# A 128-byte marker tile, and the output projection's weight sums taken beside the gates instead of beside the filters

## The chip, the cores and the metric

The kernel runs on one NeuronCore of a Trainium2 chip. The metric is the device time of one execution in microseconds. Three executions of the kernel before took 2389.43, 2389.97 and 2391.98 us (median 2389.97). All durations below come from one further execution that the hardware profiler recorded: it took 2390.31 us, of which 2388.5 us lie between the first and the last instruction of the program (the span), and about 1.8 us around them.

## The reference

One encoder layer is applied to two independent inputs of 1024 positions by 1024 channels, all in float32. Cut to what matters here:

```python
xn = rmsnorm(x, g_pre)
p = xn @ w_in                                    # 1024 x 8192
fv, fg, hv, hg, mg = split(p)
y_f = (fft2_real(fv) * silu(fg)) @ w_fourier_out
v, x1, x2 = split(short_conv(hv, w_short))
z = v
for n, gate in enumerate((x1, x2)):              # filters kf depend on weights only
    z = gate * (irfft(rfft(z, 2L) * kf[:, n]) + hyena_d[n] * z)
y_h = (z * silu(hg)) @ w_hyena_out
g_f, g_h = split(sigmoid(mg + b_merge))
out = (g_f * y_f + g_h * y_h) @ w_out            # the last projection
return x + rmsnorm(out, g_post)
```

The filters `kf` come from a small network with sine activations and a decay, and are the same for both inputs.

## The kernel before

**Number format.** A float32 product is made of three TensorE matmuls on rounded parts (`mm3` and `times`): each operand is split into a high part h (ScalarE rounds it in `split`, L167 to L172) and a low part l (VectorE or GpSimd subtracts, L180), and h·h, h·l and l·h are added in PSUM. So a stationary block h is used in two matmuls and its l in one. One TensorE line, L193, issues almost all of them; in the profile they are told apart by their tiles.

**Stages in order of time.** (1) The Fourier branch of both inputs, to about 200 us; it writes the normalized, transposed inputs to the DRAM buffers `d_x[b][k]`. (2) The filters (`phase_main`, 16 steps `i`, to about 672 us): each step makes the filter of 128 channels and writes its spectrum to DRAM, while TensorE computes parts of the input projection of input 0 (`spill_gate`, tile `pin`) between them. (3) The branches (`branches`, to about 1655 us): 32 steps of convolution by block Fourier transforms (tiles `pX`, `pT`), with the projections for v, x1, x2 (`pin`) between them; input 0 first, then input 1, whose projection weights come ready split from DRAM. (4) The gates of input 1 (`phase_tail`, to about 1912 us): 12 pairs of column tiles of `w_in`. (5) The nets (tile `pn`, to about 2208 us): the two branch projections, four times 28 products. (6) The rows: the last projection by `w_out` with the closing norm, eight pairs of row tiles, to the end.

**Seven products for eight.** Stages 4 to 6 multiply 2 by 2 blocks with seven block products. For that, sums of blocks of both operands are needed: T1 to T4 of the moving operand, and s1 to s4 of the stationary one. The T sums of input 1's data (for the gates) and of `w_out` (for the rows) are made long before their use and are kept in DRAM, in `d_t[0]` and `d_t[1]`. `block_sums` (L1132) makes one eighth of them: four loads of 128 x 512 values (256 KB) by SP's queue, three VectorE instructions, four stores of 256 KB by SP's queue. It is called eight times in the filter steps 3 to 10, alternately for `d_x[1]` and for `w_out`, in the two halves of a room that later holds the table `cinv`.

**Where tiles lie.** The pools of SBUF tiles lie one behind the other, and each tile takes its size rounded up to 32 bytes of a partition. In the program as built the constants' pool `cp` starts at byte 16512, which is 129 times 128. Its tiles take 512 + 32 + 64 + 192 + 288 + 64 + 64 + 32 = 1248 bytes, so the pool `wp` starts at byte 17760, which leaves 96 over a multiple of 128. `wp` holds eleven tiles of 2048 bytes, among them `wh` and `wl`, three buffers each of the projection's split weights (also used for the blocks 11 and 12 of the gates and rows), and last the tile `mark`, 4 bytes wide, which takes 32. So the next pool `xp` (the split inputs `x`, later reused for `oB`, `n` and other cells) starts at byte 40320, which is 315 times 128. All pools behind it (`mf`, `wa`, `wb`, `mi` of stages 2 and 3; `gs` with the rooms, `gw` with s1 to s4 and a2, `gr` in stages 4 to 6) hold tiles of multiples of 512 bytes, so their tiles start at multiples of 128 as well (but for the last, small pool of the rows). The tiles of the Fourier stage lie in pools that start where `wp` starts and are closed before.

**What sets the order.** Each engine works off one list in order. A planner makes the lists from the program order and modelled times; an instruction may move ahead of others on its engine when the plan has its operands ready. `issue_after` pins an instruction behind another one on the same engine. `mark` is written by a GpSimd copy of one column of a finished gate; it holds back one DMA of `weight_sums` per step of stage 3 until that step is done.

Of the kernel before, what the change touches and what calls it, by code (L numbers as in the profile page):

```python
# [10 lines left out]
F32R = mybir.dt.float32r  # L11
# [5 lines left out]
P = 128  # L17
# [143 lines left out]
class K:  # L161
# [824 lines left out]
    def phase_main(self, nct=8, nb=NB, nf=16):  # L986
        tc, nc, a = self.tc, self.nc, self.a
        with ExitStack() as es:
            pool = lambda n: es.enter_context(tc.tile_pool(name=n, bufs=1, reuse_waits="tile"))
            self.open_mm(es, "psm")  # L990
            mf, wa, wb, mi = pool("mf"), pool("wa"), pool("wb"), pool("mi")
            ws = Rooms(wa, wb)
            with tc.issue_after(self.fz_stored.ins):
                self.load_x(0, range(4))
            self.hid = ws.tile([P, L], F32R, tag="q", name="hid", bufs=2)
            hid = ws.tile([P, L], F32, tag="q", name="hidr", bufs=2)
            for i in range(2):
                nc.sync.dma_start(hid[64 * i:64 * i + 64].rearrange("p (n t) -> p n t", n=2),
                                  self.d_h.rearrange("(n p) t -> p n t", n=2))
            with tc.issue_after(self.third[0].ins), tc.issue_after(self.third[1].ins):  # L1000
                nc.scalar.copy(self.hid, hid)
                self.sub("dve", self.hid[64:128], hid[64:128], self.hid[64:128])
            taps = self.filter_taps(0, 0, self.filter_rates(0, 0, ws), ws)
            self.load_x(0, range(4, 8))
            self.cfw0 = mf.tile([P, 4 * P], F32, name="cfw0")
            self.cfwd = mf.tile([P, 2, 12 * P], F32R, name="cfwd")
            nc.sync.dma_start(self.cfw0, a["c_fw0"])
            nc.gpsimd.tensor_copy(self.cfwd[:, 0, 0:1], self.X[4][0][1][:, 0:1])
            nc.gpsimd.dma_start(self.cfwd, a["c_fwd"])
            plain = [(5, c) for c in range(8)] + [(6, c) for c in range(8)] + [(4, c) for c in range(NH)]  # L1010
            fill = sorted([((2 * c + 1) / len(plain), t) for c, t in enumerate(plain)]
                          + [((2 * c + 1) / max(NF, 1), (0, c)) for c in range(NF)])
            fill = [t for _, t in fill]
            rates = self.filter_rates(1, 0, ws)
            self.due = self.weight_sums()
            room = mi.tile([P, 2, INVW], F32, tag="cinv", name="sums", bufs=1).rearrange("p a b -> p (a b)")
            rows = [[self.d_x[1][k][:, 512 * h:512 * h + 512] for k in range(8) for h in range(2)],
                    [a["w_out"][k * P:(k + 1) * P, 512 * h:512 * h + 512] for k in range(8) for h in range(2)]]
            for i in range(nf):
                if 3 <= i < 11:  # L1020
                    u, k = (i - 3) % 2, (i - 3) // 2
                    self.block_sums(room[:, 2048 * u:2048 * u + 2048], u, k, rows[u])
                nxt = self.filter_taps((i + 1) % 2, (i + 1) // 2, rates, ws) if i + 1 < nf else None
                self.filter_spectrum(i % 2, i // 2, taps, ws)
                if i + 2 < nf:
                    rates = self.filter_rates(i % 2, i // 2 + 1, ws, self.rounded)
                taps = nxt
                for sec, c in fill[i * len(fill) // nf:(i + 1) * len(fill) // nf]:
                    self.spill_gate(0, sec, c, ws)
                if i == 12:  # L1030
                    self.cinv = mi.tile([P, 2, INVW], F32R, tag="cinv", name="cinv", bufs=1)
                    self.cin0 = mi.tile([P, 4 * P], F32, name="cin0")
                    nc.sync.dma_start(self.cin0, a["c_in0"])
                if 12 <= i < 15:

                    s = slice((i - 12) * INVW // 3, (i - 11) * INVW // 3)
                    nc.gpsimd.dma_start(self.cinv[:, :, s], a["c_inv"][:, :, s])
            self.branches(nb, nct, ws)

    def branches(self, nb, nct, ws):  # L1040

        tc, nc = self.tc, self.nc
        steps = []
        for b in range(nb):
            steps.append((b, 0, 0))
            for c in range(1, nct):
                steps += [(b, 0, c), (b, 1, c - 1)]
            steps.append((b, 1, nct - 1))  # L1050
        plain = list(self.PLAIN)
        Z, X, G = {}, {}, {}

        def front(i):
            b, n, c = steps[i]
            src = self.conv(1, c, ws, "v", b) if n == 0 else Z.pop(c)
            return self.conv_front(src, ws)

        def gates(i):
            b, n, c = steps[i]  # L1060
            x = self.conv(2 + n, c, ws, f"x{n + 1}", b)
            if n and b == 0:
                early = c < NH
                ps = None if early else self.inproj(4, c)
                sg = [self.wp.tile([P, 512], F32, tag="gt", name="sg", bufs=3) for q in range(2)]
                for q in range(2):
                    s = slice(512 * q, 512 * q + 512)
                    if early:
                        nc.sync.dma_start(sg[q], self.d_g[0][4][c][:, s])
                    else:  # L1070
                        nc.scalar.activation(sg[q], ps[:, s], AF.Silu)
                G[i] = sg, early
            X[i] = x

        def close(i):

            if i in G:
                sg, early = G.pop(i)
                for q in range(2):
                    s = slice(512 * q, 512 * q + 512)  # L1080
                    if early:
                        with tc.issue_after(self.rounded.ins):
                            nc.scalar.activation(sg[q], sg[q], AF.Silu)
                    self.mul("dve", X[i][:, s], X[i][:, s], sg[q])
        B = front(0)
        gates(0)
        for i, (b, n, c) in enumerate(steps):
            nxt = None
            if i + 1 < len(steps):
                nxt = front(i + 1)  # L1090
                gates(i + 1)
                if i + 2 < len(steps) and steps[i + 2][0] != steps[i + 1][0]:
                    self.load_x(steps[i + 2][0])
            y = self.conv_back(n, c, B, ws)
            close(i + 1)
            B = nxt
            for _ in range({4: 1, 3: 1, 2: 2, 1: 2}.get(len(steps) - i, 0)):
                self.spill_gate(b, *plain.pop(), ws)
            z = self.gate(n, c, y, X.pop(i))
            if self.due:  # L1100
                mark = self.wp.tile([P, 1], F32R, tag="mark", name="mark", bufs=1)
                with tc.issue_after(nc.gpsimd.tensor_copy(mark, z[:, 0:1]).ins):  # L1102
                    self.due.pop(0)()
            if n == 0:
                Z[c] = z
                continue
            nc.sync.dma_start(self.d_sh[b][c], z)
            if b == 0 and NF <= c:
                self.spill_gate(0, 0, c, ws)
        with tc.issue_after(self.ended.ins):  # L1110
            for sec, c in plain:
                self.spill_gate(1, sec, c, ws)
# [16 lines left out]

    PLAIN = [(5, 0), (5, 1), (6, 0), (6, 1), (5, 2), (5, 3), (6, 2), (6, 3)]  # L1130

    def block_sums(self, room, u, k, rows):  # L1132

        r = room.rearrange("p (a b) -> p a b", a=4)
        for q in range(4):
            self.nc.sync.dma_start(r[:, q], rows[2 * (k + 4 * (q // 2)) + q % 2])
        self.sub("dve", r[:, 0:2], r[:, 0:2], r[:, 1::2])
        self.stt("dve", r[:, 3], r[:, 0], -1.0, r[:, 3], MUL, SUB)
        self.add("dve", r[:, 2], r[:, 3], r[:, 2])
        for q, j in enumerate((0, 2, 3, 1)):  # L1140
            self.nc.sync.dma_start(self.d_t[u][j][:, k], r[:, q])

    def weight_sums(self):

# [25 lines left out]
    def phase_tail(self):  # L1170
# [10 lines left out]
        with ExitStack() as es:  # L1181
# [378 lines left out]
            for i, job in enumerate(gates):  # L1560
# [8 lines left out]
                if not end:  # L1569
                    A = prepared("g", *gates[i + 1])  # L1570
                    pa, pb, m1 = first(A, Y)
                    if i + 2 == len(gates):
                        step(-6)
                else:
                    act, dve = self.rounded.ins.engine, self.left.ins.engine
                    for s in range(2):
                        pinned(product, s)
                        step(s)
# [135 lines left out]
```

## Time and profile before

| | |
|---|---|
| median of three runs | 2389.97 us |
| the profiled execution | 2390.31 us, span 2388.5 us |
| TensorE matmul busy | 2341.1 us, 98% of the span |
| VectorE busy | 1971.1 us, 83% |
| ScalarE, GpSimd busy | 1110.1 us, 452.9 us |
| DMA | 479.71 MB, 201 GB/s in the mean |
| granted TensorE clock | 0.996 in the mean |

The groups of instructions give, for one line, engine, operation and set of tiles: the count, the busy time, the mean duration of one in ns, and the engine's idle time before them with what ended it. A tile left of the arrow is written, those right of it are read: in `pin<-x,wh` the moving operand is `x` and the stationary one `wh`. PE is a matmul, PEld the load of its stationary operand, which runs beside the matmul before. A matmul's duration is longer than the distance to the next one, since they are pipelined. The chain of work shows long runs of matmuls with their time and count, which gives that distance. The tables of stretches give each engine's busy time in a stretch, the granted clock, the share of time in which the DMA engines were busy, and GB/s.

### The profile page before, as it was taken

What the parts mean: (1) busy time and instruction counts of PE and PEld (TensorE: products, weight loads), DVE (VectorE), ACT (ScalarE), POOL (GpSimd) and SP (SyncE); (2) the same over time, 40 slices, a digit from 0 to 9 for tenths busy, and PEclk for the clock granted to TensorE, in tenths of its full rate; (3) what the DMA queues carried; (4) which work ended last, traced back from release to release, by engine and by line L of the source; (5) the groups of instructions that cost most, each with busy time, mean ns of one, the idle gap of its engine ahead of it and who ended that gap; (6) DMA issues with size and microseconds to landing.
All of it is one profiled execution on the core that took longest, in us unless ns stands there. A gap on an engine that the chain in (4) does not pass through costs nothing.

```text
span 2388.5 us, 36189 instructions
## 1 busy us (share of the span) xinstructions
PE 2341.1 (98%) x12784; PEld 2013.8 (84%) x12784; DVE 1971.1 (83%) x3430; ACT 1110.1 (46%) x2072; POOL 452.9 (19%) x428
## 2 busy tenths in 40 slices
PE   6999999999989999999999999999999999999998
PEld 5998888888878888888888888888888888888787
DVE  7775789888788999999888999997655578787987
ACT  6654557767653433334223232333443464556443
POOL 3342231222323333232000000112000000101311
PEclk9999999999999999999999999999999999999999
DMA  7636895555556567667464565455554678998654
GB/s 260 213 135 216 291 322 177 166 170 166 191 184 209 188 213 208 209 196 251 153 201 143 172 189 162 147 159 166 201 164 138 222 257 271 269 311 247 195 160 141
DMA packets 246208, 479.71 MB, mean 201 GB/s; under 512 B 24582, under 2 KB 82280, under 8 KB 245706
## 3 DMA queue, kind: packets, MB, share of 16 engines
q1 hardware_dynamic: 222013, 402.25, 51.8%
q0 software_dynamic: 23792, 75.11, 11.1%
q8 instruction: 101, 1.65, 0.3%
q14 instruction: 81, 0.66, 0.1%
q10 hardware_dynamic: 221, 0.04, 0.0%
HBM read 326.82 MB, written 177.73 MB: 211 GB/s over the span
## 4 chain that ended last, share of the span: by engine, by line
PE 49%; issue 5%; DVE 4%; DMA 3%; POOL 0%; ACT 0%; DVEq 0%; SPq 0%; POOLq 0%; ACTq 0%
PE pin L193 19%; PE pg L193 14%; PE pn L193 5%; PE pT L193 5%; PE pX L193 5%; DMA d_m<-gt 1%; PE tph L904 1%; DVE x L176 0%; DMA oB<-d_wo 0%; DMA g<-d_g 0%; DMA k<-d_k 0%; DVE wl L180 0%; DVE t L180 0%; POOL d_m L1359 0%; DVE gt L180 0%
## 5 line engine op out<-in xcount | busy, mean ns | idle before, releaser
L193 PE MATMUL pin<-x,wh 128*128 128x512 f32 x2816 | 901.9, 396 | 7.5 <-DVE x L176 7.5
L193 PEld LDWEIGHTS pin<-x,wh 128*128 128x128 f32 x2816 | 523.5, 188 | 119.7 <-issue 7.6
L193 PE MATMUL pin<-x,wl 128*128 128x512 f32 x1408 | 558.1, 397 | 0.0
L180 POOL TENSOR_TENSOR wl<-wr,wh 128x512 fp32r<-128x512 f32 x128 | 229.8, 1796 | 670.6 <-ACT wh L170 621.1
L193 PEld LDWEIGHTS pin<-x,wl 128*128 128x128 f32 x1408 | 265.0, 188 | 55.1
L193 PE MATMUL pn<-room,wh 128*128 128x512 f32 x864 | 266.5, 389 | 0.2 <-DVE room L180 0.2
L193 PEld LDWEIGHTS pn<-room,wh 128*128 128x128 f32 x864 | 162.1, 188 | 34.3 <-DVE room L180 0.6
L193 PE MATMUL pn<-room,wl 128*128 128x512 f32 x432 | 168.4, 390 | 0.6 <-DVE wl L180 0.5
L180 DVE TENSOR_TENSOR t<-pX,k 128x1024 f32<-128x1024 f32 x128 | 155.4, 1214 | 10.1 <-PE pX L193 6.8
L193 PE MATMUL pX<-bh,cfwd 128*128 128x256 f32 x768 | 162.2, 288 | 0.0
L193 PE MATMUL pT<-cinv,yh 128*128 128x256 f32 x768 | 145.6, 284 | 1.4 <-DVE T0s L180 1.4
L170 ACT CAST wh<-wr 128x512 fp32r<-128x512 f32 x128 | 79.1, 618 | 142.6 <-PE pin L193 106.2
L170 ACT CAST bh<-b 128x512 fp32r<-128x512 f32 x144 | 88.4, 620 | 113.2 <-DVE b L180 78.8
L193 PEld LDWEIGHTS pT<-cinv,yh 128*128 128x128 f32 x768 | 122.9, 190 | 8.6 <-ACT T1s L957 1.5
L193 PEld LDWEIGHTS pX<-bh,cfwd 128*128 128x128 f32 x768 | 127.1, 190 | 2.6
L1359 POOL DMA_DIRECT2D d_m<-gt x32 | 27.2, 849 | 536.4 <-DVE gt L180 498.1
L170 ACT CAST yh<-y 128x512 fp32r<-128x512 f32 x96 | 59.6, 621 | 126.9 <-DVE y L180 126.4
L180 DVE TENSOR_TENSOR bl<-b,bh 128x512 fp32r<-128x512 f32 x144 | 107.1, 748 | 7.8 <-ACT bh L170 7.7
L193 PE MATMUL pT<-cinv,yl 128*128 128x256 f32 x384 | 109.0, 284 | 0.0
L193 PE MATMUL pX<-bl,cfwd 128*128 128x256 f32 x384 | 109.0, 284 | 0.0
L1102 POOL CAST mark<-x 128x1 fp32r<-128x1 f32 x30 | 21.6, 720 | 411.2 <-DVE x L176 411.0
L180 DVE TENSOR_TENSOR y<-t 128x512 f32<-128x512 f32 x128 | 91.7, 717 | 7.3 <-PE pT L193 6.9
(359 smaller groups left out, 5154.4 us busy)
## 6 DMA issues: line engine op xcount, KB each, us to landing
k<-d_k SPq DMA_DIRECT2D x128, 512.0 KB, 4.2
wr<-in_w_in SPq DMA_DIRECT2D x128, 256.0 KB, 3.4
d_g<-gt SPq DMA_DIRECT2D x124, 256.0 KB, 2.8
wl<-d_s SPq DMA_DIRECT2D x56, 512.0 KB, 5.5
d_k<-kt SPq DMA_DIRECT2D x128, 128.0 KB, 2.3
d_k<-kt SPq DMA_DIRECT2D x64, 256.0 KB, 2.8
g<-d_g SPq DMA_DIRECT2D x64, 256.0 KB, 5.2
r<-d_g SPq DMA_DIRECT2D x60, 256.0 KB, 5.8
```

The source lines that it names most:

```text
L170: self.rounded = nc.scalar.copy(h, src)
L180: return e.tensor_tensor(out, a, b, op=op)
L193: return self.nc.tensor.matmul(out, lhsT, rhs, start=start, stop=stop, skip_group_check=shared)
L904: nc.tensor.transpose(tp[:, q * P:(q + 1) * P], eo[:, e, q], self.ident)
L1102: with tc.issue_after(nc.gpsimd.tensor_copy(mark, z[:, 0:1]).ins):
L1359: nc.gpsimd.dma_start(dst, t, accum_op=ADD)
```

## The change

`mark` becomes 32 values wide (128 bytes of a partition); the copy still writes one of them. `block_sums` takes its four tiles as a list and the two source rows, and does four VectorE instructions of 512 columns in place of three of 1024, 512 and 512. In the filters it is called four times, in the steps 3, 5, 7 and 9, for `d_x[1]` alone. The four calls for `w_out` move into the gates' loop of `phase_tail`, for the pairs 2 to 5, behind the first two block products of the next pair. They use four cells of `xp`, `x10` to `x13`, in which the second halves of the first four input tiles lay, and which no later gate reads.

```diff
@@ phase_main
-            rows = [[self.d_x[1][k][:, 512 * h:512 * h + 512] for k in range(8) for h in range(2)],
-                    [a["w_out"][k * P:(k + 1) * P, 512 * h:512 * h + 512] for k in range(8) for h in range(2)]]
             for i in range(nf):
-                if 3 <= i < 11:
-                    u, k = (i - 3) % 2, (i - 3) // 2
-                    self.block_sums(room[:, 2048 * u:2048 * u + 2048], u, k, rows[u])
+                if i in (3, 5, 7, 9):
+                    k = (i - 3) // 2
+                    r = room[:, 2048 * (k % 2):2048 * (k % 2) + 2048].rearrange("p (q n) -> p q n", q=4)
+                    self.block_sums([r[:, q] for q in range(4)], 0, k, [self.d_x[1][k + 4 * j] for j in range(2)])
@@ branches
-                mark = self.wp.tile([P, 1], F32R, tag="mark", name="mark", bufs=1)
-                with tc.issue_after(nc.gpsimd.tensor_copy(mark, z[:, 0:1]).ins):
+                mark = self.wp.tile([P, 32], F32R, tag="mark", name="mark", bufs=1)
+                with tc.issue_after(nc.gpsimd.tensor_copy(mark[:, 0:1], z[:, 0:1]).ins):
                     self.due.pop(0)()
@@ block_sums
-    def block_sums(self, room, u, k, rows):
-        r = room.rearrange("p (a b) -> p a b", a=4)
+    def block_sums(self, r, u, k, rows):
         for q in range(4):
-            self.nc.sync.dma_start(r[:, q], rows[2 * (k + 4 * (q // 2)) + q % 2])
-        self.sub("dve", r[:, 0:2], r[:, 0:2], r[:, 1::2])
-        self.stt("dve", r[:, 3], r[:, 0], -1.0, r[:, 3], MUL, SUB)
-        self.add("dve", r[:, 2], r[:, 3], r[:, 2])
+            self.nc.sync.dma_start(r[q], rows[q // 2][:, q % 2 * 512:q % 2 * 512 + 512])
+        self.sub("dve", r[0], r[0], r[1])
+        self.sub("dve", r[1], r[1], r[3])
+        self.stt("dve", r[3], r[0], -1.0, r[3], MUL, SUB)
+        self.add("dve", r[2], r[3], r[2])
         for q, j in enumerate((0, 2, 3, 1)):
-            self.nc.sync.dma_start(self.d_t[u][j][:, k], r[:, q])
+            self.nc.sync.dma_start(self.d_t[u][j][:, k], r[q])
@@ phase_tail, in the loop over the gates
                     A = prepared("g", *gates[i + 1])
                     pa, pb, m1 = first(A, Y)
+                    if 2 <= i < 6:
+                        r = [cell(xp, f"x1{2 * (i % 2) + j}", f"ws{j}") for j in range(2)]
+                        self.block_sums([r[q // 2][:, q % 2] for q in range(4)], 1, i - 2,
+                                        [a["w_out"][(i - 2 + 4 * j) * P:(i - 1 + 4 * j) * P] for j in range(2)])
```

## The prediction

> **What bounds the kernel now.** I read the busy times first, then what TensorE waited for, longest first.
>
> ```profile
> span 2388.5 us, 36189 instructions
> PE 2341.1 (98%) x12784; PEld 2013.8 (84%) x12784; DVE 1971.1 (83%) x3430; ACT 1110.1 (46%) x2072; POOL 452.9 (19%) x428
> ```
>
> ```profile
> PE tpx L359 <- DVE x L344: 11.6, 1, 11.6
> PE pin L193 <- DVE x L176: 7.5, 1, 7.5
> PE pft L193 <- DVE db L180: 1.1, 1, 1.1
> ```
>
> TensorE is busy for 98% of the span. Of its idle time 11.6 us lie at the start, where the change does nothing, and 7.5 us are one wait at the turn from the filters to the branches. So the time is nearly the sum of the distances between matmuls, and the view that matters is how far apart they follow each other. The groups of instructions, with shapes kept apart, show two classes among the matmuls of 512 columns:
>
> ```profile
> L193 PE MATMUL pin<-x,wh 128*128 128x512 f32 x2816 | 901.9, 396 | 7.5 <-DVE x L176 7.5
> L193 PE MATMUL pg<-x,wh 128*128 128x512 f32 x176 | 55.3, 395 | 0.0
> L193 PE MATMUL pg<-oB,wh 128*128 128x512 f32 x120 | 37.7, 395 | 0.0
> L193 PE MATMUL pg<-x,wa 128*128 128x512 f32 x24 | 5.6, 389 | 0.0
> L193 PE MATMUL pg<-x,s4h 128*128 128x512 f32 x96 | 29.5, 389 | 0.0
> L193 PE MATMUL pg<-oB,s4h 128*128 128x512 f32 x64 | 19.7, 389 | 0.0
> L193 PE MATMUL pn<-room,wh 128*128 128x512 f32 x864 | 266.5, 389 | 0.2 <-DVE room L180 0.2
> L193 PEld LDWEIGHTS pin<-x,wh 128*128 128x128 f32 x2816 | 523.5, 188 | 119.7 <-issue 7.6
> L193 PEld LDWEIGHTS pn<-room,wh 128*128 128x128 f32 x864 | 162.1, 188 | 34.3 <-DVE room L180 0.6
> ```
>
> With the same moving tile `x`, the matmul takes 395 ns with `wh` of the pool `wp` and 389 with `wa` or `s4h` of `gw`; with `oB` it is again 395 and 389. (`wh` under `pn` is another tile, in `gw` and `xp`.) The load of the stationary block takes 188 ns in both classes. The chain gives the distances: 27.76 us for 119 `pin` is 233.3 ns, 5.44 us for 24 `pg` of the other class is 226.7 ns, a difference of 6.6.
>
> ```profile
> 1659.04 27.76 PE pin L193 x119
> 1917.05 5.44 PE pg L193 x24
> ```
>
> What tells the classes apart is where the tiles lie: `wp` starts 96 bytes over a multiple of 128, and all else on a multiple. That is the link to `mark`, which shifts every pool behind `wp`.
>
> On the last point the Trainium skill speaks against any effect. Its page "SBUF — State Buffer" (section Operand start alignment, and the 16-byte cachelines of its specifications) asks only for a start at a multiple of the element size, and a shift by 32 bytes crosses no other number of 16-byte lines; its page "TensorE: Matmul & The Clock Gate" (Part 2, Step-by-step) says that loading the next weights takes no read bandwidth from the running matmul. By these pages the two classes would be one; the trace has 395 and 389 ns. The same page's distance for 512 columns (Back-to-back issue gap) would be 512/2.4 + 2.5 = 216 ns, an estimate; the trace has 226.7 and 233.3.
>
> **The change, part 1: `mark`.** Its tile takes 128 bytes for 32, so every tile behind `wp` starts 96 bytes later: 96 over a multiple of 128, as `wp`'s tiles do. The copy still writes one value and costs what it cost. No instruction is added. There are two readings of the two classes, which the trace of before can't part, since there the moving tile always lies on a multiple.
>
> Reading A: what costs 6.6 ns is that the two operands lie differently. After the change all pairs lie alike, and the `wp` class falls to 226.7. Reading B: what costs is a stationary tile off the multiple. Then the `wp` class stays, and the other class rises to 233.3. I lean to A, since the load of a `wp` block is not longer (188 and 188 ns); it is the matmul running beside it that is longer, so it looks like two streams in each other's way, and that depends on both addresses. That is an argument, not a proof.
>
> How many matmuls each reading moves, by stage (matmuls that touch `pin`, then all):
>
> ```profile
> 200.00:672.00 472.00, 363.26 (x1508) 278.04 (x1509) 0.00 (x0) 33.17 (x60) 1.00 0.66 213
> 672.00:1100.00 428.00, 278.00 (x1111) 203.28 (x1109) 58.48 (x46) 26.67 (x25) 0.99 0.65 199
> 1100.00:1655.00 555.00, 367.84 (x1483) 269.69 (x1483) 63.75 (x50) 34.35 (x37) 1.00 0.55 171
> 1655.00:1912.00 257.00, 29.43 (x125) 22.92 (x123) 0.00 (x0) 3.21 (x6) 1.00 0.56 185
> ```
>
> ```profile
> 1100.00:1655.00 555.00, 555.00 (x3275) 487.06 (x3274) 502.54 (x834) 168.46 (x306) 48.74 (x50) 1.00 0.55 171
> 1655.00:1912.00 257.00, 257.00 (x1136) 211.06 (x1135) 147.08 (x223) 105.20 (x178) 4.17 (x3) 1.00 0.56 185
> 1912.00:2208.00 296.00, 295.77 (x1304) 244.31 (x1303) 232.75 (x248) 178.51 (x232) 20.39 (x24) 1.00 0.86 271
> 2208.00:2389.00 181.00, 169.48 (x736) 137.28 (x735) 151.53 (x283) 77.14 (x159) 40.16 (x24) 0.98 0.54 166
> ```
>
> Reading A: 1508, 1111, 1483 and 125 `pin`, and in gates and rows 176 + 120 with the high part shown above and half as many with the low part, 444 in all. Times 6.6 ns: 10.0 + 7.3 + 9.8 + 0.8 + 2.9 = 30.8 us. Not all of it reaches the end, since a faster TensorE meets VectorE in the branches of input 0:
>
> ```profile
> 800.00:900.00 100.00, 100.00 (x590) 87.72 (x589) 98.06 (x155) 36.16 (x66) 41.90 (x44) 1.00 0.67 206
> 900.00:1000.00 100.00, 98.65 (x595) 86.95 (x594) 96.44 (x150) 33.41 (x60) 29.43 (x36) 1.00 0.68 210
> 1000.00:1100.00 100.00, 100.00 (x592) 87.72 (x591) 100.00 (x163) 37.46 (x70) 36.88 (x36) 1.00 0.68 196
> ```
>
> There VectorE is busy for 294.5 of 300 us, so 5.5 are left, and TensorE would need about 5 less (7.3 times 300/428). I take 3 of these as lost, and 1 more in 1100 to 1655, where VectorE has 502.5 of 555. That leaves 27. Between nothing lost and all of the 7.3 lost, the ends are 31 and 23.
>
> Reading B: of the 3176 matmuls behind 1655 us, 125 `pin` and 444 with `wp` tiles stay; the rest, some 2600, rise by 6.6 ns: 17 us more, and TensorE never waits there for long, so all of it shows.
>
> The matmuls of 256 columns I cost at nothing under both. Their durations lie close together wherever their tiles lie (the Fourier pools hold tiles at odd starts):
>
> ```profile
> L193 PE MATMUL pT<-cinv,yl 128*128 128x256 f32 x384 | 109.0, 284 | 0.0
> L193 PE MATMUL pse<-seq,oo 128*128 128x258 f32 x48 | 7.1, 283 | 0.0
> L193 PE MATMUL pso<-seq,oo 128*128 128x258 f32 x48 | 7.7, 288 | 0.7 <-DVE sst L180 0.7
> ```
>
> For 3000 of them, 1 ns either way is 3 us either way. DMAs into shifted tiles could change too; tiles of `wp` are loaded today at the same offset, so I take nothing and allow 2 us either way.
>
> **Part 2: the sums for `w_out` leave the filters.** The rows for the tile `sums`, and the stretches in which they lie:
>
> ```profile
> L180 DVE TENSOR_TENSOR sums<-sums x16: 675/950/1227, 259.3 to 333.5; 128x1024 f32<-128x1024 f32 x8, 128x512 f32<-128x512 f32 x8
> L176 DVE SCALAR_TENSOR_TENSOR sums<-sums x8: 673/682/691, 260.5 to 330.2; 128x512 f32<-128x512 f32 x8
> DMA to landing us min/median/max: 3.3/4.8/7.0
> ```
>
> ```profile
> 300.00:350.00 50.00, 48.90 (x259) 40.86 (x258) 41.81 (x84) 25.56 (x54) 14.59 (x9) 1.00 0.99 331
> 350.00:400.00 50.00, 49.54 (x277) 42.18 (x276) 48.12 (x112) 36.22 (x86) 12.78 (x7) 1.00 0.62 192
> ```
>
> Four calls go: 16 loads, 16 stores (8.4 MB) from SP's queue, and on VectorE 4 x (1.23 + 0.68 + 0.68) = 10.3 us. They go from where the DMA engines are 99% busy. But TensorE is idle there for 1.10 + 0.46 = 1.6 us only, so the gain lies between 0 and 1.6; I take 1, since the one wait that has a name (`db`, 1.1 us) is for VectorE, which they load. The four calls that stay cost 4 x 0.1 more on VectorE (four instructions of 0.68 for 2.59), hidden under TensorE's work.
>
> The wait of 7.5 us at the turn to the branches is 350 us later. VectorE was not full in between, so the missing 10 us don't pass on by themselves; but the planner lays its lists anew, and that wait may shrink to nothing or come twice: 7.5 us either way, nothing in the sum.
>
> **Part 3: they come to the gates.** Four pairs, each 19 us long (224.8 us of the chain's `pg` for 12 pairs), get 4 x 0.68 = 2.7 us on VectorE, four loads and four stores on SP's queue. VectorE is busy there for 147 of 257 us and the DMA engines for 0.56, so there is room; TensorE, busy for all of 257, is the cover. What is queued behind: on VectorE, in order, the sums hold up the evacuation of the gates' PSUM if they wait for a load; on SP's queue, a store that waits for VectorE holds up the next pair's loads of `w_in`. In the filters a load took 4.8 us to land. The cells are free from the end of the last projection, so the first two pairs' loads can go long before; only the third and fourth wait for a store. Nothing can be gained, since TensorE has no idle time there to lose. Ends: 0, and 2 x 4.8 = 10 us if VectorE stood still for both landings with no cover. I take 0.5, near the end that the row of the stretch gives.
>
> Sum on the profiled execution: 2390.3 - 27 - 1 + 0.5 = 2362.8, so 2363. That execution lies 0.3 us above the median of the runs, which changes nothing here.
>
> **The rivals.** *B, the stationary tile alone:* 2390.3 + 17 - 0.5 = 2407. For it: the stationary tile's place is all that differs between rows with the same moving tile, so it is the shorter account. Against it: the load's 188 ns. It decides as soon as the 512-column matmuls of the nets stand 233 ns apart. *C, no effect of the shift:* `wp`'s matmuls are slow for something else that stays with `wp` (its low addresses, the DMAs into it): 2390.3 - 0.5 = 2390, with the planner's 7.5 either way. For it: `wp` itself doesn't move. The pages quoted above give the same time by their own reasoning. *D, the gates become late:* the stores on SP's queue delay the loads of the third and fourth pair's successors by a landing and the sums (4.8 + 2.7 = 7.5 us each, 15 us in all); with A 2378, without it 2405. It decides once TensorE waits for more than 5 us in 1655 to 1912. Against it are the idle 110 us of VectorE there. *E, the moving tile off the multiple costs as well:* another 6.6 ns for 7250 matmuls, 2455. No row speaks for it.
>
> **How the numbers follow.** A 0.46, C 0.20, B 0.26, D 0.05, E 0.03. Likeliest: A, 2363; its own range is 2350 (nothing lost on VectorE, the wait at the turn gone) to 2378. The range over the cases must take in C and B to leave out no more than 2 in 10: 2352 to 2410. Below 0.2% (4.8 us, about what a measurement can tell from no change) under 2390: A, and a fifth of C and D: 0.51. Within: most of C, 0.16. Above: B, E, the rest of C and D: 0.33.
>
> **What would show it.** A: `pin<-x,wh` falls from 396 to 389 ns and `pg<-x,wh` with it, while `pn<-room,wh` stays at 389. B: `pn` and the s tiles rise to 395, `pin` stays. C: both stay. Part 2: no `sums` from `w_out` before 400 us, TensorE's idle time in 300 to 400 under 1.6. Part 3: tiles `ws` in the gates, TensorE still busy for all of that stretch. The prediction is wrong if the two classes don't move, or the other way; and too low if VectorE holds the branches by more than 4 us.

## The result, and the profile after

The changed kernel takes 2387.59 us (median of 22 runs, 2383.93 to 2393.20), the kernel before beside it 2391.74 (22 runs): a ratio of 0.9985, with a 95% interval of 0.9979 to 0.9990. By this ratio that is 3.6 us less, and not the 27 that I forecast. The profiled execution took 2390.22 us, 0.1 us less than the one profiled before, so its views show what moved inside the kernel and not the whole gain.

The page of the changed kernel, its span and busy times:

```profile
span 2388.4 us, 36206 instructions
PE 2339.0 (98%) x12784; PEld 2019.5 (85%) x12784; DVE 1967.7 (82%) x3438; ACT 1118.6 (47%) x2080; POOL 446.4 (19%) x428
```

By the prediction TensorE's busy time was to fall by some 27 us; it fell by 2. The groups of instructions of the changed kernel, with the two classes of 512-column matmuls of the prediction:

```profile
L193 PE MATMUL pin<-x,wh 128*128 128x512 f32 x2816 | 900.3, 395 | 0.0
L193 PE MATMUL pin<-x,wl 128*128 128x512 f32 x1408 | 556.8, 396 | 0.0
L193 PE MATMUL pn<-room,wh 128*128 128x512 f32 x864 | 266.2, 389 | 0.0
...
L193 PE MATMUL pT<-cinv,yl 128*128 128x256 f32 x384 | 108.9, 284 | 0.0
...
L193 PE MATMUL pg<-x,wh 128*128 128x512 f32 x176 | 55.3, 395 | 0.0
...
L193 PE MATMUL pg<-x,s4h 128*128 128x512 f32 x96 | 29.6, 390 | 0.0
```

`pin` was at 396 and 397 and is at 395 and 396; `pg<-x,wh` was and is at 395; the other class stays at 389 or 390. The chain of work gives the distances (start, time, count):

```profile
1659.61 27.66 PE pin L193 x119
1687.28 224.92 PE pg L193 x984
...
1917.63 5.44 PE pg L193 x24
```

27.66 us for 119 is 232.4 ns, where it was 233.3. Over 4224 `pin` that is 3.8 us, as much as the whole gain. The fast class is at 5.44/24 = 226.7 ns as before. So neither class changed sides. The rest of the change, in the views in which the prediction looked for it, the waits of TensorE first (total, times, longest):

```profile
PE tpx L359 <- DVE x L344: 11.7, 1, 11.7
PE pXf L193 <- DVE b L180: 5.5, 1, 5.5
...
PE pn L765 <- DVE acc L180: 2.2, 1, 2.2
```

The wait of 7.5 us at the turn to the branches is now one of 5.5 us by another matmul, and a wait of 2.2 us in the filters is new. Then stretches of time of the changed kernel, with the busy time of each engine, the granted clock, the DMA share and GB/s:

```profile
300.00:350.00 50.00, 50.00 (x273) 43.08 (x272) 41.22 (x98) 33.55 (x73) 13.31 (x10) 1.00 0.72 229
350.00:400.00 50.00, 50.00 (x275) 43.18 (x275) 41.52 (x99) 35.37 (x79) 9.75 (x7) 1.00 0.56 175
...
1655.00:1912.00 257.00, 257.00 (x1135) 211.48 (x1134) 156.23 (x239) 105.49 (x178) 8.51 (x3) 1.00 0.64 218
```

In the filters the DMA share fell from 0.99 to 0.72 in the stretch where it had been full, and TensorE's 1.6 us of idle time there are gone. They are not gained, though: with the new wait of 2.2 us TensorE is idle for 2.8 us in all between 205 and 672 us, where before it was 1.6. In the gates VectorE and the DMA engines carry what was added (147 to 156 us, 0.56 to 0.64), and TensorE is still busy for all of the 257 us. The moved sums themselves, tile `ws` of the changed kernel:

```profile
L180 DVE TENSOR_TENSOR ws<-ws x8: 682/684/693, 1697.4 to 1723.0; 128x512 f32<-128x512 f32 x8
...
its engine sat idle before it (us, times) until:
  DMA ws<-in_w_out: 0.9, 2
...
DMA to landing us min/median/max: 2.2/6.0/9.3
```

VectorE stood still for 0.9 us in all for their landings.

### The profile page after: what moved, and what is told of

The parts are those of the page before. It is cut to its first block, busy times and chain, and to the rows that moved or that the text cites. A ratio compares the mean times of both kernels' runs of the same rounds, so it can differ in the third digit from the quotient of the medians.

```text
span 2388.4 us, 36206 instructions
## 1 busy us (share of the span) xinstructions
PE 2339.0 (98%) x12784; PEld 2019.5 (85%) x12784; DVE 1967.7 (82%) x3438; ACT 1118.6 (47%) x2080; POOL 446.4 (19%) x428
## 4 chain that ended last, share of the span: by engine, by line
PE 55%; DVE 4%; DMA 1%; issue 1%; ACT 0%; POOL 0%; DVEq 0%; SPq 0%; POOLq 0%; ACTq 0%
PE pin L193 19%; PE pg L193 14%; PE pn L193 12%; PE pT L193 5%; PE pX L193 5%; PE tph L904 1%; DMA xr<-in_x 1%; DVE x L176 0%; DMA d_m<-gt 0%; DMA k<-d_k 0%; DVE t L180 0%; DVE b L180 0%; DVE y L180 0%; DVE wl L180 0%; DVE o L176 0%
## 5 line engine op out<-in xcount | busy, mean ns | idle before, releaser
L180 POOL TENSOR_TENSOR wl<-wr,wh 128x512 fp32r<-128x512 f32 x128 | 223.5, 1747 | 696.1 <-ACT wh L170 661.3
```

The costliest lines, as they stand in the source:

```text
L180: return e.tensor_tensor(out, a, b, op=op)
```

## The experiments

The question was why `pin` stayed slow. Theory P: what sets the pace is the difference between the starts of the stationary and the moving tile, but modulo 512 bytes, not 128. In the kernel before this difference is 32 for the `wp` class and 0 for the other; after the change it is 128 and 0. Theory W: `wp`'s matmuls are slow for something that stays with `wp` (the prediction's rival C). No kernel below leaves out or changes any part of the computation.

**Mark alone, and the sums alone.** The kernel before with part 1 only:

```diff
-                mark = self.wp.tile([P, 1], F32R, tag="mark", name="mark", bufs=1)
-                with tc.issue_after(nc.gpsimd.tensor_copy(mark, z[:, 0:1]).ins):
+                mark = self.wp.tile([P, 32], F32R, tag="mark", name="mark", bufs=1)
+                with tc.issue_after(nc.gpsimd.tensor_copy(mark[:, 0:1], z[:, 0:1]).ins):
```

> The kernel before with mark 128 bytes wide and nothing else (part 1 alone; the order of every engine's instructions is that of before; nothing is left out). Theory P (a matmul of 512 columns runs at 226.7 ns only where its stationary and its moving tile start at the same remainder modulo 512 bytes; 32 bytes apart and 128 bytes apart are both wrong): the pin matmuls stay at 232 to 233 ns, and the time is 1 to 5 us under before, as the whole of the change was (3.6 us). Theory W (the weights of wp are slow for something that stays with that pool, its place or the writes into it, and the offset means nothing): pin stays at 233.3 ns, time within 1 us of before, and the 3.6 us come from the moved sums. Reading A of the prediction (apart by a multiple of 128 is enough) would give pin at 227 ns and 2363; the result of the whole change speaks against it.

The changed kernel with that edit undone:

> The changed kernel with mark back at 4 bytes in its 32-byte slot (parts 2 and 3 alone: the sums of the weights beside the gates, those of the data beside the filters; the order of every engine's instructions is that of the changed kernel; nothing is left out). Theory P: pin at 233.3 ns as before, time within 2 us of before (the moved sums cost and gain nothing that lasts). Theory W: 3.6 us under before, like the whole change.

Measured: 2389.17 us, 0.9989 of before (0.9980 to 0.9998), and 2389.19 us, 0.9991 (0.9982 to 1.0000). The same run of `pin` in the chains, mark alone first, then the sums alone:

```profile
1656.00 27.66 PE pin L193 x119
```

```profile
1657.93 27.76 PE pin L193 x119
```

232.4 ns with the wide mark, 233.3 without, whatever the sums do. So the 0.9 ns belong to `mark`, and reading A with its multiple of 128 is out. Each half is worth some 2 us (2.6 and 2.2 by the ratios); the sum of 4.8 agrees with the 3.6 within the intervals. W's expectation, all of it from the sums, is not met by `mark`'s half. That placement can have a large effect these two runs don't show yet.

**No difference at all.** The changed kernel with `mark` in the pool of constants, ahead of `wp`: `wp` moves up by 32 bytes, and all tiles behind it start at the same remainder as its own.

```diff
-        self.ones = cp.tile([P, 2], F32, name="ones")
+        self.ones = cp.tile([P, 2], F32, name="ones"); self.mark = cp.tile([P, 1], F32R, name="mark")
...
-                mark = self.wp.tile([P, 32], F32R, tag="mark", name="mark", bufs=1)
-                with tc.issue_after(nc.gpsimd.tensor_copy(mark[:, 0:1], z[:, 0:1]).ins):
+                with tc.issue_after(nc.gpsimd.tensor_copy(self.mark, z[:, 0:1]).ins):
```

> The changed kernel with mark taken out of wp and put into the pool of constants ahead of it, so that the tiles behind wp lie at the same remainder modulo 512 as those of wp (apart by 0 instead of 128 bytes); order of instructions as in the changed kernel, nothing left out. Theory P: pin's 128x512 matmuls fall from 232.4 to 226.7 ns and their weight-load rows from 396 to 389, 4224 x 5.7 ns = 24 us, less 0 to 5 us where VectorE (94% busy in 800 to 1100 us) becomes the limit: 2364 to 2371 us, 0.988 to 0.992 of before. Theory W: pin stays at 232 to 233 ns, 2385 to 2392 us.

Measured: 2370.45 us, 0.9908 of before (0.9891 to 0.9925). Groups, chain and stretches of this kernel:

```profile
span 2362.9 us, 36206 instructions
PE 2318.3 (98%) x12784; PEld 2016.4 (85%) x12784; DVE 1966.6 (83%) x3438; ACT 1119.0 (47%) x2080; POOL 449.0 (19%) x428
...
L193 PE MATMUL pin<-x,wh 128*128 128x512 f32 x2816 | 889.0, 391 | 0.0
```

```profile
1637.86 27.00 PE pin L193 x119
1664.86 223.04 PE pg L193 x984
```

```profile
900.00:1000.00 100.00, 98.57 (x590) 87.42 (x589) 98.68 (x153) 34.35 (x64) 35.43 (x42) 1.00 0.69 208
```

The run of `pin` is at 226.9 ns and the gates begin at 1664.9 us, 22 us earlier than before. (This execution took 2364.98 us, the shortest of the four; the difference of the medians is 20.7.) W is out. The mean of all `pin` stays 2 ns above the fast class (391 to 389), which I come back to.

**A difference of 64 and of 96 bytes.** The changed kernel with a narrower mark:

```diff
-                mark = self.wp.tile([P, 32], F32R, tag="mark", name="mark", bufs=1)
+                mark = self.wp.tile([P, 16], F32R, tag="mark", name="mark", bufs=1)
```

> The changed kernel with mark 64 bytes wide (the tiles behind wp 64 bytes off wp's remainder instead of 128; order of instructions as in the changed kernel, nothing left out). Theory P: 64 bytes apart is no match either, pin at 232 to 233.5 ns, time 2385 to 2392 us. Theory W: the same, so this run gives the pace at a third offset and rules out that only 32 and 128 are bad ones. Rival to both (the best offset lies between): pin at 227 to 230 ns, 2365 to 2378 us.

and `[P, 24]`:

> The changed kernel with mark 96 bytes wide, a difference of 96 bytes. From 0, 32, 64 and 128 bytes (228, 233.3, 229, 232.4 ns) no rule is clear. If odd multiples of 32 are the bad ones and 128 is bad for another reason, 233 ns and about 2388 us; if the pace goes up evenly from 64 to 128, about 231 ns and 2380 us.

Measured: 2373.80 us, 0.9922 (0.9906 to 0.9938), at 64 bytes, which P had wrong; and 2391.95 in a single run at 96, beside 2391.23 for before. The chains, 64 bytes first:

```profile
1641.99 27.24 PE pin L193 x119
```

```profile
1660.95 27.76 PE pin L193 x119
```

228.9 ns and 233.3, the latter as the first of its two cases had it. So P's first form, in which only an equal remainder is fast, falls: 64 bytes cost 2 ns, and 32, 96 and 128 cost 5.5 to 6.4. From here on P says only that the difference sets the pace.

**The difference or the place.** All runs so far moved the tiles as well as their difference. Two kernels part these: the changed kernel with mark at 32 bytes in `wp` again and a pad ahead, so that `wp` lies at the remainder 384 (fast in the run without a difference) and the rest at 416; and the kernel without a difference with everything at 480.

```diff
-        self.ones = cp.tile([P, 2], F32, name="ones")
+        self.ones = cp.tile([P, 2], F32, name="ones"); cp.tile([P, 8], F32, name="pad")
...
-                mark = self.wp.tile([P, 32], F32R, tag="mark", name="mark", bufs=1)
+                mark = self.wp.tile([P, 1], F32R, tag="mark", name="mark", bufs=1)
```

> The changed kernel with mark back at 32 bytes in wp, and a pad of 32 bytes in the pool of constants: wp's tiles move to the absolute remainder that was fast in the run at 0 bytes (384), the tiles behind to the one of the run at 64 bytes (416), and the difference is that of before, 32. Theory P (difference decides): pin at 233 to 233.5 ns as before, about 2388 us. Rival Q (the absolute remainder of the stationary tile decides: 352 slow, 384 fast): pin at 227 to 228 ns, about 2366 us. Rival R (that of the moving tile decides; 384 gave 233.3 and 227 already, so R alone can't be): pin at 229 ns, about 2373 us.

```diff
-        self.ones = cp.tile([P, 2], F32, name="ones")
+        self.ones = cp.tile([P, 2], F32, name="ones"); self.mark = cp.tile([P, 32], F32R, name="mark")
...
-                mark = self.wp.tile([P, 32], F32R, tag="mark", name="mark", bufs=1)
-                with tc.issue_after(nc.gpsimd.tensor_copy(mark[:, 0:1], z[:, 0:1]).ins):
+                with tc.issue_after(nc.gpsimd.tensor_copy(self.mark[:, 0:1], z[:, 0:1]).ins):
```

> The changed kernel with a mark of 128 bytes in the pool of constants: stationary and moving tiles both at remainder 480 of 512, the moving tile's place of the changed kernel, difference 0. Theory P: pin at 227 to 228 ns, 2364 to 2372 us. Rival Q (absolute remainder of the stationary tile): 480 is a third place, neither 352 nor 384, so 227 only by chance; 229 to 233 ns, 2373 to 2390 us.

Measured: 2386.44 us in a single run, and 2371.86, 0.9918 (0.9905 to 0.9931). The chains in the same order:

```profile
1656.51 27.76 PE pin L193 x119
```

```profile
1644.10 27.00 PE pin L193 x119
```

Shifted by 32 with the difference of 32 kept: 233.3 ns, as before. Shifted by another 96 with no difference: 226.9, as in the run without a difference. In the places tried, the place adds nothing and the difference decides; rival Q is out.

**The placement without the moved sums.** The kernel before with `mark` in the pool of constants (the edit of the run without a difference, on the kernel before).

> The kernel before with mark in the pool of constants and nothing else: tiles apart by 0 instead of 32 bytes, the sums of the weights still beside the filters. If the placement alone makes the gain (theory P, as corrected by the run at 64 bytes: the pace goes with the difference of the two tiles' starts modulo 512, 0 best), pin falls from 233.3 to 227 to 228 ns, 4224 x 5.3 to 6 ns = 22 to 25 us: 2365 to 2370 us, 0.989 to 0.992 of before, within 3 us of the changed kernel with mark at the same place (2370). If the moved sums are needed for it (with pin faster the filters would be held by VectorE, which still sums the weights there), 2374 to 2382.

Measured: 2374.69 us, 0.9929 (0.9917 to 0.9941). The page and the chain of this kernel:

```profile
L193 PE MATMUL pin<-x,wh 128*128 128x512 f32 x2816 | 889.8, 392 | 7.7 <-DVE x L176 7.5
```

```profile
1644.64 27.00 PE pin L193 x119
```

Most of the gain comes by the placement alone. The 2374.7 lie at the lower end of what was expected if the moved sums were needed for the rest, and the two kernels with the sums moved lie 3 to 4 us lower (2370.45, 2371.86). Their intervals overlap with this one's, so whether the sums are worth more once `pin` is fast stays open. The wait of 7.5 us at the turn is here again, as it is with mark alone; it goes with the sums in the filters.

**The opposite test: making the fast class slow.** The kernel before with 32 bytes of padding at the head of the pool `gw`, so that the stationary tiles of the gates' sums, until now without a difference, lie 32 bytes behind their moving tiles' remainder, on the other side than `pin`'s.

```diff
-            gs, gw, gr, gt, op = pool("gs"), pool("gw"), pool("gr"), pool("gt"), pool("op")
+            gs, gw, gr, gt, op = pool("gs"), pool("gw"), pool("gr"), pool("gt"), pool("op"); gw.tile([P, 8], F32, name="pad", bufs=1)
```

> The kernel before with a pad of 32 bytes at the head of the pool gw, which holds the stationary tiles of the gates' data matmuls: 1464 matmuls of 512 columns in the gates and the last projection (the classes pg of s1 to s4 and a2, and 264 of the 1296 pn of room), until now at the same remainder as their moving tiles, come 32 bytes off it, on the other side than pin. Nothing is left out. Theory P (any pair is slowed by its difference): these classes go from 390 to about 396 ns in their group rows and from 226.8 to 233 ns apart, 1464 x 6.3 ns = 9 us, 2400 us, 1.004 of before. Theory W (something of wp's own): all stay at 390, 2391 us, 1.000.

Measured: 2399.28 us, 1.0038 of before (1.0024 to 1.0052), 8.8 us more. Groups and chain of this kernel, and behind them the same piece of the chain of before:

```profile
L193 PE MATMUL pg<-x,wh 128*128 128x512 f32 x176 | 55.3, 395 | 0.0
L193 PE MATMUL pg<-room,s1h 128*128 128x512 f32 x160 | 50.5, 397 | 1.2 <-ACT u L1243 1.1
L193 PE MATMUL pg<-room,s3h 128*128 128x512 f32 x160 | 50.3, 396 | 0.0
...
L193 PE MATMUL pg<-x,s4h 128*128 128x512 f32 x96 | 30.1, 395 | 0.0
...
L193 PE MATMUL pn<-n,wh 128*128 128x512 f32 x32 | 9.9, 389 | 0.0
```

```profile
1690.48 229.52 PE pg L193 x984
```

```profile
1686.81 224.80 PE pg L193 x984
```

Of the 984 `pg` in the gates, 264 use `wp` and were slow already; the other 720 take 4.7 us more than before (there 224.80 us for the 984), which is 6.6 ns each. `pn<-n,wh`, whose tiles didn't part, stays at 389. The effect is not peculiar to `wp`, and it has about the same size on either side.

## Why the prediction was wrong, point by point

**Part 1, reading A: the step that failed.** "After the change all pairs lie alike": the step took a start alike modulo 128 for enough. Its term of 30.8 us measured 2.6 us with the wide mark alone (0.5 to 4.8 by the interval): at 128 bytes apart `pin` fell by 0.9 ns and not by 6.6. With no difference, the placement alone gave 17 us. The runs give, by the chain's `pin` for each difference (remainder of 512):

| bytes apart | ns between matmuls | kernels |
|---|---|---|
| 0 | 226.9 | mark in the constants, three kernels |
| 32 | 233.3 | before; sums alone; shifted with 32 kept |
| 64 | 228.9 | mark of 64 bytes |
| 96 | 233.3 | mark of 96 bytes |
| 128 | 232.4 | the change; mark alone |

The mechanism behind A, that the pace depends on how the two operands lie to each other, held: the moved difference moved the pace, the moved place didn't. Its size held too: 6.4 ns between 0 and 32, where I had 6.6. What I had no row for was the period. In the trace of before every fast pair was alike modulo 128 and modulo 512 at once, since all those tiles are multiples of 512 bytes, and every slow pair was 32 off; the two can't be told apart there. I took the smaller period without a reason, and gave the result of that choice 0.46. The runs rule out 128 as the period; whether it is 512 or 256 they don't tell, as no pair of the table lies 256 bytes apart. A reading "alike modulo 512 only" would have left `pin` slow at 128 and given about 2390.

**Rival C** had the time (2390 less the half microsecond; 2387.6 measured) and the wrong reason. The shift does have an effect, 0.9 ns here and 6.4 with no difference. The same goes for the Trainium skill's page "TensorE: Matmul & The Clock Gate" (Part 2, Step-by-step), where loading the next weights takes no read bandwidth from the running matmul: by this the difference should cost nothing, and the runs show that it does: with 32 bytes each 512-column matmul is 6.4 ns further from the next, at a load that still takes 188 or 189 ns. Whether it is read bandwidth that is lost, no run shows.

**Rivals B and E** are out by the changed kernel itself: its fast pairs, both tiles now 96 bytes off the multiple of 128, kept their 226.7 ns. **D** is out: TensorE was busy for all of 1655 to 1912.

**The 4 us lost to VectorE.** This can be read in the kernels where A's effect did take place. In full, 4224 `pin` times 6.4 ns are 27 us. By the starts of the matmuls in the traces, the stretch from the first `pin` to the gates became shorter by 20.3 us in the run "No difference at all", and by 16.7 in the profiles of the two other kernels without a difference. So 7 to 10 us were lost ahead of the gates, and not 4. But they were not lost as I had it: TensorE is idle for no longer in 900 to 1000 us (98.57 busy, 98.65 before). Most of the loss is in the pace. In the first of these kernels the starts of all `pin` stand 228.3 ns apart in the mean, 1.4 more than in the run of 119, which over 4224 is 6 us; they stand 227.7 apart in 200 to 300 us, where VectorE is busy for 65%, and 229.3 in 1000 to 1100, where it is busy for 99.8%, with some 231 to 236 among the 227. It is largest where VectorE is fullest, but it is there all along; what delays these was not tried.

**Part 2** was 1 us, with ends at 0 and 1.6: TensorE's 1.6 us of idle time in 300 to 400 are gone, but the new wait of 2.2 us in the filters takes as much. The sums alone measure 2.2 us less than before, with an interval from 4.3 to 0. The wait at the turn, which I had counted at nothing with 7.5 either way, gave 2 of its 7.5 us. **Part 3** was 0.5 us, and the chain's 984 `pg` took 224.92 us for 224.80. **The 256-column matmuls**, at nothing under all readings, stayed where they were, 284 ns for `pT<-cinv,yl` before and after. That is no test of an effect on them: both of these operands lie behind `wp`, so the shift moved them together.

## What to carry to other kernels

Where a group row shows two durations for one shape, list the start of both operands before you explain it, and write down every modulus by which the rows sort; where several sort them alike, each is a reading of its own, and the change's new remainder has to be run through each. A marker or a flag of a few bytes belongs ahead of all large pools or behind them, not at the end of one: here taking it out of `wp`, with the sums moved, gave 2370.45 us, 0.9908 of before (0.9891 to 0.9925), some six times the gain of the change as made. When TensorE is busy for 98% of the span, a gain or a loss of 3% per matmul shows in no wait; here it showed in the distance between matmuls, and as 6 ns in the durations of the group rows.

## What the hardware showed that I had not expected

In this kernel the pace of back-to-back 512-column matmuls with a new stationary block each depends on the difference of the two operands' starts (modulo 512 bytes, or 256), as in the table: not evenly (64 bytes cost 2 ns, 32 and 96 cost 6.4), and for 32 with the stationary tile on either side. With a difference of 0 the distances are 226 and 227 ns almost without exception in the gates; with 32 nearly all lie between 229 and 235. The figures of the table are means of a pattern that repeats: in the run of 119 `pin` at 64 bytes the distances go round in threes, about 226, 229 and 232 ns, at 96 bytes about 230, 232 and 238, and at 128 in rounds of seven between 228 and 241. Which of the two reads waits for the other, and on what, stays open: these runs only show when it happens. A difference of 256 bytes wasn't tried.
